# A feed-forward net in three-pass float32: block-product chunks that add onto sums in PSUM, one weight sum made by adding transfers, and one more such chunk in the first net

## The chip, the cores and the metric

The kernel runs on one core of one Trainium2 chip. The metric is the time of one execution on the device in microseconds (us); lower is better. The median of three runs is compared.

## The reference, cut to what matters

Two layers of a small model on 256 tokens of width 1024, all float32. Each layer has two gated feed-forward nets, a token mixer and an attention over 256 memory rows, each followed by a layer norm. The change touches the four feed-forward nets alone.

```python
D_FF = 2816
def swiglu(x, w_gate, w_up, w_down):
    return (jax.nn.silu(x @ w_gate) * (x @ w_up)) @ w_down
for l in range(2):
    h = layer_norm(ALPHA * h + 0.5 * swiglu(h, ffn1_gate[l], ffn1_up[l], ffn1_down[l]), ...)
    ...   # mixer, attention over mem
    h = layer_norm(ALPHA * h + 0.5 * swiglu(h, ffn2_gate[l], ffn2_up[l], ffn2_down[l]), ...)
```

## The kernel before

A product of float32 values is made on TensorE (PE) in three passes: every operand is split into a high part (rounded to the float32r type) and a low part (the rest), and `high*high`, `high*low` and `low*high` are summed in PSUM. `split` (L60 to L62) makes the parts: a cast on ScalarE (ACT, L61) and a subtraction on VectorE (DVE, L62). All weights pass through it: SP loads a tile `raw` of 128x1024 (six buffers), ACT writes `whi`, DVE writes `wlo` (eight buffers each), and PE multiplies with them. So DVE can be at most eight tiles ahead of PE. One weight tile serves 12 matmuls of 512 columns in a plain chunk, and 6 in a block-product chunk.

A net walks over the 2816 hidden columns in chunks: five of 512 and a last one of 256. For a plain chunk (`hidden`), gate and up products take 96 matmuls; `activate` and `gated` leave `silu(gate)*up` in `sg`, and `turn` brings it into the layout that the down product wants, by four transfers (`dealt`), two transposes on DVE and a split. The down product of a chunk is done in two halves by `both(c, u)`, 24 matmuls each, one and two chunks later: at chunk `c` the kernel issues `both(c - 2, 1)` and `both(c - 1, 0)`.

A block-product chunk (`by_seven`, L568 on) treats gate and up of one chunk as four blocks: two halves of the 1024 input columns by gate and up, and the 256 tokens as two tiles of 128. It takes the four block results out of seven products instead of eight, so 84 matmuls instead of 96. For that it needs sums of weight blocks (L597, four sums, each of two 128x1024 tiles, made in place on DVE), sums of input blocks (`blocks_of_x`, once per net), and sums of the seven results (`put`, L619, on DVE). `w00`, `w01`, `w11` and `w10` are the blocks as loaded. Chunks 2 and 4 of a net are of this kind (`sevens`), but in the first net of the first layer (`early` given) only chunk 4.

The first net is special in another way: its chunks 1 and 2 are laid beside the preparation of the memory rows. The memory lands in the tiles `spare0` and `spare1` (32 small transfers issued by POOL, L193), is transposed on DVE (L202) and split into `mT`; small parameters come in through `spare2` and are worked out with some twenty small DVE instructions. `spare0`, `spare1`, `spare2`, `lng` and `lnb` are also the tiles in which `by_seven` puts weight blocks.

The order of instructions on each engine is fixed when the program is built, by a list scheduler with a model of its own; on the chip every engine runs its list strictly in order, and waits where an operand is late. `tc.issue_after` ties the preparation work to places in the list.

Of the kernel before, what the change touches and what calls it, by code (L numbers as in the profile page):

```python
# [17 lines left out]
P = 128  # L18
# [28 lines left out]
def model(ctx: ExitStack, tc: tile.TileContext, t: dict, out: bass.AP):  # L47
# [16 lines left out]
    def load(src, k0, nk, c0, ncol, fine=False):  # L64
# [4 lines left out]
        for a in range(k0, k0 + nk, step):  # L69
# [6 lines left out]
            for b in range(0, step, part):  # L76
                loads.append(nc.sync.dma_start(
                    raw[b // half][:, b % half : b % half + part, :],
                    src[(a + b) * P : (a + b + part) * P, c0 : c0 + ncol].rearrange("(k p) c -> p k c", p=P),
                ))  # L80
# [21 lines left out]
    def product(o, w, x, start, stop):  # L102
        x = x.rearrange("p (h c) -> p c h" if len(x.shape) == 2 else "p r (h c) -> p r c h", h=2)
        o = o.rearrange("p (c h) -> p c h" if len(o.shape) == 2 else "p r (c h) -> p r c h", h=2)
        nc.tensor.matmul(o, w, x, start=start, stop=stop)  # L105
# [23 lines left out]
    def mm_rows(o, xh, xl, wh, wl, start, stop):  # L129
        product(o, xh, wh, start, False)  # L130
        product(o, xh, wl, False, False)
        product(o, xl, wh, False, stop)
# [50 lines left out]
    def load_memory(mp, behind):  # L183
# [14 lines left out]
        def later():  # L198
            for n in range(2):
                for k in range(0, 4, 2):  # L200
                    turned = mp.tile([P, 2, SEQ], F32, tag="up", name="turned")
                    nc.vector.transpose(  # L202
                        turned.rearrange("p k t -> p (k t)"), m[n][:, k : k + 2].rearrange("p k b j -> p (k b j)")
                    )
                    d = slice(4 * n + k, 4 * n + k + 2)
                    split(mTh[:, d, :], mTl[:, d, :], turned)
# [193 lines left out]
    def ffn(l, name, n, pend=None, last=False, early=None):  # L400
        gate, up, down = (t[f"{name}_{x}"][l] for x in ("gate", "up", "down"))
        with tc.tile_pool(name="ffn", bufs=2, reuse_waits="tile") as fp:
# [24 lines left out]
            def ordered(v):  # L427
                return v.rearrange("p (a k j) -> p k a j", a=4, j=32)

            def by_two(v, o):  # L430
                o = o.rearrange("p (n a j m) -> p m n a j", n=2, a=4, m=2)
                return [(ordered(v)[:, 2 * m : 2 * m + 2], o[:, m]) for m in range(2)]

            def activate(s, i, og):
                for v, o in by_two(s[:, i, :], og):
                    nc.scalar.activation(v, o, AF.Silu)

            def gated(s, i, ou):
                for v, o in by_two(s[:, i, :], ou):
                    nc.vector.tensor_tensor(v, o, v, op=ALU.mult)  # L440
# [5 lines left out]
            def turn(s):  # L446
                ah, al = act_tiles()
                x = fp.tile([P, 4, NT, P], F32, tag="dealt", name="dealt", bufs=1)
                for a in range(4):
                    nc.sync.dma_start(x[a * 32 : a * 32 + 32], s[:, :, a * P : (a + 1) * P])  # L450
                for i in range(NT):
                    d = fp.tile([P, 4, P], F32, tag="up", name="square")
                    nc.vector.transpose(
                        d.rearrange("p k (b r) -> p b k r", b=4), x[:, :, i, :].rearrange("p b (k j) -> p b k j", k=4)
                    )
                    split(ah[:, :, tok(i)], al[:, :, tok(i)], d)
# [111 lines left out]
            def by_seven(c0, bx):  # L568
# [19 lines left out]
                w00 = block(gate, 0, pieces("spare0", "spare1"))  # L588
                w01 = block(up, 0, pieces("lng", "lnb"))
# [20 lines left out]
                def run(o, x, w):  # L610
                    for k in range(4):
                        wh, wl = w.at(k, slice(0, CHUNK))
                        mm_rows(o, x[0][:, k, :], x[1][:, k, :], wh, wl, k == 0, k == 3)

                def half_sum():
                    return fp.tile([P, 4, P], F32, tag="up", name="half").rearrange("p k t -> p (k t)")

                def put(o, a, op, b):
                    nc.vector.tensor_tensor(halves(o), sums(a), halves(b), op=op)  # L619

                s = activations()
                g = [s[:, i, :] for i in range(NT)]
                o = [acc((P, CHUNK)) for _ in range(4)]
                run(o[0], part_of_x(0, 0), parts_of(w00))
                nc.scalar.copy(halves(g[0]), sums(o[0]))
                run(o[2], bx[0], parts_of(w00, w01))
                run(o[1], bx[1], parts_of(w00, w11))
                e = half_sum()
                put(e, o[1], ALU.add, g[0])
                run(o[3], bx[2], parts_of(w01, w11))  # L630
                put(g[1], o[3], ALU.add, e)
                f = half_sum()
                put(f, o[2], ALU.subtract, g[1])
                put(e, o[2], ALU.subtract, e)
                o = [acc((P, CHUNK)) for _ in range(3)]
                run(o[0], bx[3], parts_of(w11))
                run(o[1], part_of_x(0, 1), parts_of(w10))
                run(o[2], part_of_x(1, 1), parts_of(w00, w10))


                def left():
                    put(e, o[0], ALU.add, e)
                    for i in range(NT):
                        put(g[i], o[1 + i], ALU.add, g[i])
                    s = fp.tile([P, NT, CHUNK], F32, tag="spare2", name="sg", bufs=1)
                    for i, u in enumerate((e, f)):
                        v = ordered(s[:, i, :])
                        nc.scalar.activation(v, g[i].rearrange("p (k a j) -> p k a j", a=4, j=32), AF.Silu)
                        nc.vector.tensor_tensor(v, v, u.rearrange("p (k a j) -> p k a j", a=4, j=32), op=ALU.mult)
# [571 lines left out]
```

## Time and profile before

| | |
|---|---|
| median of three runs | 1071.56 us (1070.53 to 1072.04) |
| span of the profiled execution | 1068.8 us |
| median less that span | 2.8 us (1071.56 - 1068.8) |
| TensorE busy / its granted clock | 99% of the span / 0.998 |
| VectorE, ScalarE, GpSimd busy | 89%, 60%, 6% |
| DMA queue of SP | 228.49 MB, 64.8% of 16 engines |

The profile is of one execution. A matmul's row is longer than the time it keeps the engine from starting the next one, because matmuls are pipelined; the distance between starts is what counts, and the chain of waits gives it per stage. Views used: the page, the list of waits, the chain of waits in order of time, the timeline of one engine (start, duration, instruction, how many merged, and the idle time before it with what ended it), the groups by line and shape, busy time by stretches (windows), and the DMA issues.

### The profile page before, as it was taken

How to read it: one execution, taken by the hardware profiler on the slowest of the kernel's cores; microseconds unless marked ns; L12 is line 12 of the kernel's file. 1: busy time of each engine (PE TensorE's matmuls, PEld its weight loads, DVE VectorE, ACT ScalarE, POOL GpSimd, SP SyncE). 2: the span in 40 equal slices, each digit the busy share in tenths (PEclk: the TensorE clock that was granted, in tenths of full speed). 3: DMA queues.
4: the chain of work that ended last, by engine and by line, in shares of the span. 5: the costliest groups of instructions: out<-in, count | busy, mean ns of one | idle time of the engine just before them, and what ended most of it. 6: DMA issues, size and time to landing. Idle time of an engine off the chain costs nothing.

```text
span 1068.8 us, 16312 instructions
## 1 busy us (share of the span) xinstructions
PE 1059.3 (99%) x5966; PEld 937.7 (88%) x5966; DVE 946.3 (89%) x1318; ACT 642.4 (60%) x916; POOL 66.4 (6%) x114
## 2 busy tenths in 40 slices
PE   9999999999999999999999999999999999999997
PEld 7888888889899888888888888888898998888886
DVE  6977997998988799999799999788989787999996
ACT  7555664666557565656575557566764665656660
POOL 9700001000000000000000000010000000000000
PEclk9999999999999999999999999999999999999999
DMA  9997484755574575848675865856536665759461
GB/s 362 262 307 256 129 288 165 249 176 174 170 278 167 178 252 194 290 167 218 238 272 184 256 254 183 290 179 216 196 126 213 241 227 181 257 156 334 134 223 40
DMA packets 130895, 231.90 MB, mean 217 GB/s; under 512 B 9408, under 2 KB 48608, under 8 KB 130816
## 3 DMA queue, kind: packets, MB, share of 16 engines
q1 hardware_dynamic: 129024, 228.49, 64.8%
q0 software_dynamic: 1216, 1.20, 0.5%
q8 instruction: 47, 0.77, 0.3%
q10 hardware_dynamic: 576, 1.18, 0.3%
q14 instruction: 32, 0.26, 0.1%
HBM read 216.15 MB, written 1.05 MB: 203 GB/s over the span
## 4 chain that ended last, share of the span: by engine, by line
PE 99%; DMA 0%; DVE 0%; issue 0%; DVEq 0%
PE acc L105 65%; PE dn L105 31%; PE acc L172 1%; PE dn L923 1%; PE dn L982 0%; DMA h<-in_x_dram 0%; PE acc L491 0%; PE dn L981 0%; PE dn L971 0%; PE acc L1047 0%; PE dn L888 0%; DVE h L358 0%; DVE h L353 0%; PE dn L472 0%; DVE st L338 0%
## 5 line engine op out<-in xcount | busy, mean ns | idle before, releaser
L61 ACT CAST whi<-raw 128x1024 fp32r<-128x1024 f32 (+1 forms) x438 | 442.9, 1042 | 197.5 <-DVE raw L597 54.9
L62 DVE TENSOR_TENSOR wlo<-raw,whi 128x1024 fp32r<-128x1024 f32 (+1 forms) x438 | 515.7, 1209 | 32.6 <-ACT whi L61 29.0
L105 PE MATMUL acc<-whi,xT 128*128 128x512 f32 x1032 | 312.9, 380 | 0.0
L105 PEld LDWEIGHTS acc<-whi,xT 128*128 128x128 f32 x1032 | 195.1, 189 | 27.5
L105 PE MATMUL acc<-wlo,xT 128*128 128x512 f32 x516 | 195.6, 379 | 0.0
L105 PE MATMUL acc<-xT,whi 128*128 128x512 f32 x576 | 142.3, 383 | 0.2
L105 PE MATMUL dn<-whi,ah 128*128 128x512 f32 x346 | 131.5, 380 | 0.0
L105 PE MATMUL dn<-wlo,ah 128*128 128x512 f32 x346 | 131.2, 379 | 0.0
L105 PE MATMUL dn<-whi,al 128*128 128x512 f32 x346 | 131.2, 379 | 0.0
L105 PEld LDWEIGHTS acc<-xT,whi 128*128 128x128 f32 x576 | 104.0, 190 | 12.5 <-ACT whi L61 0.7
L105 PEld LDWEIGHTS acc<-wlo,xT 128*128 128x128 f32 x516 | 97.5, 189 | 13.8
L105 PE MATMUL dn<-whi,xT 128*128 128x512 f32 x288 | 87.9, 381 | 0.0
L105 PEld LDWEIGHTS acc<-xT,wlo 128*128 128x128 f32 x576 | 75.5, 191 | 3.9
L105 PE MATMUL acc<-xT,wlo 128*128 128x256 f32 x576 | 75.9, 275 | 0.0
L105 PEld LDWEIGHTS dn<-whi,al 128*128 128x128 f32 x346 | 65.4, 189 | 9.2
L105 PEld LDWEIGHTS dn<-wlo,ah 128*128 128x128 f32 x346 | 65.4, 189 | 9.2
L105 PEld LDWEIGHTS dn<-whi,ah 128*128 128x128 f32 x346 | 65.4, 189 | 9.1
L350 POOL TENSOR_TENSOR rs<-rs,nhalf 128x1 f32<-128x1 f32 x16 | 14.9, 930 | 833.6 <-DVE rs L346 598.1
L597 DVE TENSOR_TENSOR raw<-raw 128x1024 f32<-128x1024 f32 x56 | 66.2, 1217 | 0.4
L105 PEld LDWEIGHTS dn<-whi,xT 128*128 128x128 f32 x288 | 54.4, 189 | 7.7 <-DVE xT L62 0.3
L105 PE MATMUL dn<-wlo,xT 128*128 128x512 f32 x144 | 54.6, 379 | 0.0
L332 DVE SCALAR_TENSOR_TENSOR h<-h,dn 128x512 f32<-128x512 f32 x31 | 21.2, 683 | 32.9 <-PE dn L105 32.9
(234 smaller groups left out, 1277.5 us busy)
## 6 DMA issues: line engine op xcount, KB each, us to landing
raw<-in_ffn_up_dram SPq DMA_DIRECT2D x88, 512.0 KB, 5.3
raw<-in_ffn_down_dram SPq DMA_DIRECT2D x88, 512.0 KB, 6.6
raw<-in_ffn_gate_dram SPq DMA_DIRECT2D x84, 512.0 KB, 5.1
raw<-in_w_in_dram SPq DMA_DIRECT2D x48, 512.0 KB, 4.7
dealt<-sg SPq DMA_DIRECT2D x80, 128.0 KB, 4.7
raw<-in_ca_k_dram SPq DMA_DIRECT2D x16, 512.0 KB, 4.9
raw<-in_w_out_dram SPq DMA_DIRECT2D x16, 512.0 KB, 4.5
raw<-in_ca_v_dram SPq DMA_DIRECT2D x16, 512.0 KB, 5.3
```

What stands on the lines that cost most here:

```text
L61: nc.scalar.copy(hi, src)
L62: lows.append(nc.vector.tensor_tensor(lo, src, hi.bitcast(F32), op=ALU.subtract))
L105: nc.tensor.matmul(o, w, x, start=start, stop=stop)
L172: nc.tensor.transpose(pt[:, k, :], src[:, (4 * j + k) * P : (4 * j + k + 1) * P], unit)
L332: nc.vector.scalar_tensor_tensor(v, v, ALPHA / scale, sums(y[i][n]), op0=ALU.mult, op1=ALU.add, accum_out=None if junk is None else st[:, ...
L350: nc.gpsimd.tensor_tensor(rs, rs, nhalf[:, 0:1], op=ALU.pow)
L597: nc.vector.tensor_tensor(r[i], r[i], plus[i], op=ALU.add)
L923: nc.tensor.matmul(o[g, hh, :], kc[:, hh, g], x, start=True, stop=True)
```

## The change

It does five things.

1. In `by_seven`, products that end in the same result are added in PSUM: one bank is written by four of the seven products and read three times in between by ACT copies (`taken`), a second one is written by two. `put` is left with three uses instead of seven. Matmuls onto a bank that was read must come after that read.
2. The last weight sum, `w00 + w10`, is made by two adding transfers that POOL issues (`accum_op=ALU.add`): they read the `w10` rows from HBM a second time and add them onto `w00` in SBUF.
3. The first net's chunk 3 becomes a block-product chunk too: `sevens` is `(3, 4)` there. `w00` and `w01` swap homes from one such chunk to the next.
4. `both(c - 2, 1)` is issued inside `by_seven`, between the fifth and the sixth product, and `both(c - 1, 0)` before the chunk is finished (`left`).
5. The rows of the down weights are dealt out so that the results can be read in another order; `activate`, `gated` and the split in `turn` become one instruction where they were two. The tile tag `up` has one buffer of 128x1024 instead of two of 128x512, and `turned` (the transposed memory) uses it.

```diff
@@ load
-    def load(src, k0, nk, c0, ncol, fine=False):
+    def load(src, k0, nk, c0, ncol, fine=False, dealt=False):
+                if dealt:
+                    c, u = divmod(a // 2, 2)
+                    at = slice(c * CHUNK + 2 * P * b, c * CHUNK + 2 * P * (b + 1))
+                    rows = src[at, c0 : c0 + ncol].rearrange("(p u) c -> p u c", u=2)[:, u, :]
+                    loads.append(nc.sync.dma_start(to[:, 0, :], rows))
@@ load_memory, later
-                    turned = mp.tile([P, 2, SEQ], F32, tag="up", name="turned")
+                    turned = mp.tile([P, NT, CHUNK], F32, tag="up", name="turned", bufs=1)[:, 0, :]
@@ ffn
-                for v, o in by_two(s[:, i, :], og):
-                    nc.scalar.activation(v, o, AF.Silu)
+                nc.scalar.activation(ordered(s[:, i, :]), in_order(og), AF.Silu)
@@ turn
+                d = fp.tile([P, NT, 4, P], F32, tag="up", name="square", bufs=1)
                 for i in range(NT):
-                    d = fp.tile([P, 4, P], F32, tag="up", name="square")
                     nc.vector.transpose(
...
-                    split(ah[:, :, tok(i)], al[:, :, tok(i)], d)
+                split(*(y.rearrange("p k (i t) -> p k i t", i=NT) for y in (ah, al)), d)
@@ by_seven
+                homes = [("spare0", "spare1"), ("lng", "lnb")]
+                turn_of = sevens.index(c0 // CHUNK) % 2
...
-                o = [acc((P, CHUNK)) for _ in range(4)]
-                run(o[0], part_of_x(0, 0), parts_of(w00))
-                nc.scalar.copy(halves(g[0]), sums(o[0]))
-                run(o[2], bx[0], parts_of(w00, w01))
-                run(o[1], bx[1], parts_of(w00, w11))
-                put(e, o[1], ALU.add, g[0])
-                run(o[3], bx[2], parts_of(w01, w11))
-                put(g[1], o[3], ALU.add, e)
-                put(f, o[2], ALU.subtract, g[1])
-                put(e, o[2], ALU.subtract, e)
-                o = [acc((P, CHUNK)) for _ in range(3)]
-                run(o[0], bx[3], parts_of(w11))
-                run(o[1], part_of_x(0, 1), parts_of(w10))
-                run(o[2], part_of_x(1, 1), parts_of(w00, w10))
+                o = [acc((P, CHUNK)) for _ in range(2)]
+                run(o[0], part_of_x(0, 0), parts_of(w00))
+                taken(s[:, 0, :], o[0])
+                run(o[1], bx[0], parts_of(w00, w01))
+                run(o[0], bx[1], parts_of(w00, w11), True)
+                for i in range(2):
+                    k = 4 + 2 * i
+                    nc.gpsimd.dma_start(
+                        w00[i], gate[k * P : (k + 2) * P, c0 : c0 + CHUNK].rearrange("(k p) c -> p k c", p=P),
+                        accum_op=ALU.add,
+                    )
+                taken(e, o[0])
+                o.append(acc((P, CHUNK)))
+                run(o[2], part_of_x(0, 1), parts_of(w10))
+                run(o[0], bx[2], parts_of(w01, w11), True)
+                put(s[:, 0, :], o[2], ALU.add, s[:, 0, :])
+                nc.scalar.activation(s[:, 0, :], s[:, 0, :], AF.Silu)
+                taken(f, o[0])
+                between()
+                put(f, o[1], ALU.subtract, f)
+                run(o[1], bx[3], parts_of(w11), True)
+                run(o[0], part_of_x(1, 1), parts_of(w00), True)
                 def left():
-                    put(e, o[0], ALU.add, e)
-                    for i in range(NT):
-                        put(g[i], o[1 + i], ALU.add, g[i])
...
+                    activate(s, 1, o[0])
+                    put(e, o[1], ALU.subtract, e)
+                    nc.vector.tensor_tensor(s, s, ef, op=ALU.mult)
                     return turn(s)
@@ ffn
-            sevens = (2, 4) if early is None else (4,)
+            sevens = (2, 4) if early is None else (3, 4)
@@ chunk loop
                 if c > 0:
-                    if c > 1:
+                    if c > 1 and c not in sevens:
                         both(c - 2, 1)
+                    if c < len(chunks) - 1:
+                        both(c - 1, 0)
                     if c in sevens:
                         acts.append(left())
-                    if c < len(chunks) - 1:
-                        both(c - 1, 0)
```

More of the change, by code (lines that the diff above doesn't have):

```diff
@@ L586, in block @@
                     return to
-                w00 = block(gate, 0, pieces("spare0", "spare1"))
-                w01 = block(up, 0, pieces("lng", "lnb"))
+                homes = [("spare0", "spare1"), ("lng", "lnb")]
+                turn_of = sevens.index(c0 // CHUNK) % 2
+                w00 = block(gate, 0, pieces(*homes[turn_of]))
+                w01 = block(up, 0, pieces(*homes[1 - turn_of]))
                 w11 = block(up, 1, pieces("raw", "raw"))
@@ L638, in by_seven @@
[L638 to L649 removed]
+                ef = fp.tile([P, NT, CHUNK], F32, tag="up", name="halves", bufs=1)
```

62 lines of the change are left out of this document (31 added, 31 removed).

## The prediction

> **What bounds the kernel now.** I read the page first, then the list of waits for TensorE (PE), then the chain of waits in order of time, then the VectorE (DVE) timeline of the stages that the change rebuilds.
>
> ```profile
> span 1068.8 us, 16312 instructions
> PE 1059.3 (99%) x5966; PEld 937.7 (88%) x5966; DVE 946.3 (89%) x1318; ACT 642.4 (60%) x916; POOL 66.4 (6%) x114
> PEclk9999999999999999999999999999999999999999
> ```
>
> ```profile
> PE dn L472 <- DVE kTh L467: 1.5, 1, 1.5
> PE acc L491 <- DMA h<-in_x_dram: 0.5, 1, 0.5
> ```
>
> PE waits for 2.0 us in the whole run, all of it at the start. Everything else is issue of matmuls at full clock. So only fewer matmuls can shorten the run, and any wait put on PE lengthens it by its full length. The chain gives the rate (start, length, count):
>
> ```profile
> 75.27 10.36 PE dn L105 x48
> 85.63 20.72 PE acc L105 x96
> 106.35 10.36 PE dn L105 x48
> 116.71 18.13 PE acc L105 x84
> 134.84 10.36 PE dn L105 x48
> ```
>
> 18.13/84 is 0.216 us a matmul. These are the first net's chunk 3 (plain, 96 matmuls from 85.63, then two down halves) and chunk 4 (block products, 84 from 116.71). PE never waits here, but DVE only just keeps up. Its timeline in chunk 4:
>
> ```profile
> 99.75 1.22 DVE L62 TENSOR_TENSOR wlo<-raw,whi 128x1024 fp32r<-128x1024 f32 x1 [0.51 <-ACT whi L61]
> ...
> 115.08 2.36 DVE L597 TENSOR_TENSOR raw<-raw 128x1024 f32<-128x1024 f32 x2
> 117.35 1.30 DVE L453 STREAM_TRANSPOSE square<-dealt 128x512 f32<-128x512 f32 x2
> 118.57 1.19 DVE L62 TENSOR_TENSOR wlo<-raw,whi 128x1024 fp32r<-128x1024 f32 x1
> 119.67 1.28 DVE L62 TENSOR_TENSOR al<-square,ah 128x512 fp32r<-128x512 f32 x2
> 120.88 5.76 DVE L62 TENSOR_TENSOR wlo<-raw,whi 128x1024 fp32r<-128x1024 f32 x5
> 126.55 0.69 DVE L619 TENSOR_TENSOR half<-acc,sg 128x512 f32<-128x512 f32 x1
> 127.15 2.35 DVE L62 TENSOR_TENSOR wlo<-raw,whi 128x1024 fp32r<-128x1024 f32 x2
> 129.42 0.69 DVE L619 TENSOR_TENSOR sg<-acc,half 128x512 f32<-128x512 f32 x1
> 130.02 1.22 DVE L62 TENSOR_TENSOR wlo<-raw,whi 128x1024 fp32r<-128x1024 f32 x1
> ```
>
> The row at 99.75 splits this chunk's first tile: ready at 100.97, wanted at 116.71, a lead of 15.7 us. The row at 130.02 splits the first tile of the down half behind the 84 products: ready at 131.24, wanted at 134.84, a lead of 3.6. One block-product chunk has eaten 12 us of DVE's lead, because a tile there keeps PE busy for 6 matmuls (1.3 us) but costs DVE a subtraction and more than half an addition. Between them DVE is never idle. The steps from start to start are what I count with: 5.67/5 = 1.135 for a 128x1024 subtraction, 2.27/2 = 1.135 for an addition, 0.60 for a 128x512 one, 1.22 for a pair of transposes.
>
> **The change part by part.** *Matmuls.* The first net's chunk 3 drops from 96 to 84: 12 x 0.216 = 2.6 us off PE. The other block-product chunks keep their 84. This is the whole gain on the path, since no other stage has PE idle time to win back.
>
> *DVE.* Each block-product chunk loses two additions (2 x 1.135) and four of seven `put`s (4 x 0.60), about 4.7 us with the merged instructions. In the six chunks of the other three nets, where DVE was never late before, that is more lead and worth nothing. In the first net, chunk 3 gains 6 splits and 6 additions (13.6 us), and stands directly in front of chunk 4, which used to begin with the full lead. So I count DVE's list, in its built order, against PE.
>
> The count starts where before and after are alike, at the memory's transposes:
>
> ```profile
> 66.20 1.30 DVE L202 STREAM_TRANSPOSE turned<-m 128x512 f32<-128x512 f32 x2
> 67.43 1.19 DVE L62 TENSOR_TENSOR wlo<-raw,whi 128x1024 fp32r<-128x1024 f32 x1
> 68.53 1.28 DVE L62 TENSOR_TENSOR mT<-turned,mT 128x512 fp32r<-128x512 f32 x2
> 69.73 1.30 DVE L202 STREAM_TRANSPOSE turned<-m 128x512 f32<-128x512 f32 x2
> 70.95 1.18 DVE L62 TENSOR_TENSOR wlo<-raw,whi 128x1024 fp32r<-128x1024 f32 x1
> 72.06 1.29 DVE L62 TENSOR_TENSOR mT<-turned,mT 128x512 fp32r<-128x512 f32 x2
> 73.26 3.49 DVE L62 TENSOR_TENSOR wlo<-raw,whi 128x1024 fp32r<-128x1024 f32 x3
> 76.67 1.41 DVE L440 TENSOR_TENSOR sg<-acc,sg 128x256 f32<-128x256 f32 x4
> ```
>
> Stretch A, from 66.20 to the second tile of chunk 3's `w00`: four transposes (2.44), four `mT` subtractions (2.4), four splits and two additions (6.8), two `gated` instructions (1.2), 12.9 us in all, so 79.1. But `spare0` and `spare1`, where `w00` lands, hold the memory until it is transposed, and `turned` now has one buffer, so each transpose waits for the cast and subtraction of the one before. The last transpose ends near 73.6; SP can only then issue the second `w00` load; two down tiles stand behind the first one in SP's queue. With the row for such a load, and for the cast that follows it,
>
> ```profile
> raw<-in_ffn_gate_dram SPq DMA_DIRECT2D x84, 512.0 KB, 5.1
> m<-in_mem_dram POOLq DMA_DIRECT2D x32, 32.0 KB, 5.8
> ```
>
> ```profile
> L61 ACT CAST whi<-raw 128x1024 fp32r<-128x1024 f32 x430 | 438.2, 1049 | 197.2 <-DVE raw L597 54.9 <-PE dn L105 53.5 <-PE acc L105 35.5
> L625 ACT COPY sg<-acc 128x512 f32<-128x512 f32 x7 | 4.1, 579 | 0.0
> ```
>
> 73.6 + 5.1 + 1.05 + 1.135 = 80.9; the load may be a little quicker, and I take 80.7. It cannot be under 77.0: in the built order the two `gated` instructions stand in front, the second needs the `up` products of chunk 2, which end at 75.27, and takes 0.60 before the 1.135.
>
> Stretch B, from there to the first down tile that PE uses inside chunk 4. The built DVE list holds 29 subtractions, 10 additions and one product of 128x1024 (40 x 1.135 = 45.4), four transposes (2.44), four `put`s (2.4) and 15 tiny parameter instructions. Those filled, with two splits (2.27), the time between these rows, so they cost up to 1.9; I take 1.5:
>
> ```profile
> 89.93 0.18 DVE L268 COPY prm<-acc 128x32 f32<-128x32 f32 x1
> ...
> 94.14 2.36 DVE L62 TENSOR_TENSOR wlo<-raw,whi 128x1024 fp32r<-128x1024 f32 x2
> ```
>
> Sum 51.7. One microsecond more for waits on ScalarE (ACT), which now does three copies a chunk in its queue of casts, one of them behind the table load for the parameters' `Exp`: 52.7. The tile is ready at 80.7 + 52.7 = 133.4.
>
> PE would want it at 85.63 + 28.49 (84 + 48 matmuls of chunk 3) + 10.36 (four products of chunk 4) = 124.5. The built PE order puts three matmuls of that down half ahead of the fifth product, so PE stands still for them. PE therefore loses 133.4 - 124.5 = 8.9 us over the two chunks. Bounds: 77.0 + 51.7 = 128.7 gives 4.2; 2 us more of waits on DMA or ACT give 10.9. Behind this point chunk 5 restores the lead, as before.
>
> *PE on ACT's copies.* A product that adds onto a bank waits for the copy out of it, with one product (12 x 0.216 = 2.6 us) to hide it. A cast already begun (1.05) and the copy (0.58) fit. In the first net's chunk 3 the copy stands behind casts that wait for DVE's additions, so this wait comes out of the same 8.9. In chunk 2 of the later nets the copy stands behind a cast that needs a buffer PE frees 1.3 us into that product: 1.3 + 1.05 + 0.58 = 2.9, 0.3 too late, but the built order has two matmuls of another product in between (0.43). Zero, bounded by two such places in three chunks, 6 x 0.3 = 1.8.
>
> *The adding transfers.* Each waits on POOL for DVE's last split of the old `w00`; behind it on POOL stand only the layer norms' powers (L350), due much later. Before ACT casts the sum, DVE has 12 instructions in between, some 12 us in every chunk. The trace has no adding transfer; its neighbours land in 5.1 (512 KB, SP) and 5.8 us (32 KB, POOL). I take twice 5.1, hidden, so nothing. If the cover fails, each microsecond beyond 12 counts eight times.
>
> *Edits with one answer.* Merged `activate`, `gated` and `turn` splits save fixed costs on DVE and ACT, off the path. The dealt down rows keep 4 KB runs. `lng` and `lnb` load later, behind the last `w00` split, still over 15 us before use. Moving `both` keeps PE's count and gives DVE a rest in mid chunk; it is in the count.
>
> Sum: 1068.8 - 2.6 + 8.9 = 1075.1 for the span, 1077.9 by the median's offset of 2.8. I say 1078.0.
>
> **Rivals.** *Lead suffices (faster).* If DVE's tiles came in time, the 2.6 us would stand: 1069.0. For it: DVE idles several times before 86 us. Against: its list is strictly ordered, and even the floor above leaves 4.2 us. It decides only if stretch B costs under 43 us. *Small stall.* Between the floor and a little below (2 to 4.5 us lost), within 0.2% of before: 1071.5. It needs quick landings and no ACT waits. *The clock drops.* A long gap could cost PE its rate, as at the start of the run, where five matmuls of 512 columns took
>
> ```profile
> 1.52 2.50 PE L472 MATMUL dn<-kTh 128*128 128x512 f32 x5 [1.52 <-DVE kTh L467]
> ```
>
> 0.50 us each. The gap at 124.5 is one of about 3 us or more; some 16 matmuls at twice 0.216 would add 3.5: 1081.5. [...] *Adding transfers late.* At 15 us each, 3 x 8 = 24 us more: 1102. POOL issued its 32 loads while DVE was nearly saturated and they landed in 5.8, so I give it little.
>
> **How the numbers follow.** About 0.2% (2.1 us) is what can be told from no change here. The forecast 0.64, clock drop 0.11, adding transfers 0.05: slower 0.80. Small stall 0.10: same. Lead suffices 0.10: faster. The range reaches from the floor of the forecast with its quickest landings, 1071.56 - 2.6 + 4.2 = 1073.2, rounded down to 1072.5, to 1082.5, which holds the clock drop and the 1.8 of the copies; outside are the faster case and the late transfers.
>
> **What would show it.** Right: PE waits of 6 to 11 us in all between 88 and 140 us, named by DVE `wlo` (L62) or ACT; DVE without idle time from 66 to 133; from there on the chain as before, shifted; PE 12 matmuls shorter. In the other nets no PE wait over 0.3. Wrong: no PE wait in that stretch (lead suffices), ACT casts waiting on the adding transfers, or a granted clock below 1 there.

## The result, and the profile after

The changed kernel takes 1079.9 us (median of 4, 1079.7 to 1084.1), the kernel before in the same runs 1071.8 (1070.5 to 1072.5): a ratio of 1.0088, 95% interval 1.0072 to 1.0105. It is slower by 8.1 us. The prediction was 1078.0 in a range of 1072.5 to 1082.5. The profiled execution took 1079.9, 2.0 above its span. Its page:

```profile
span 1077.9 us, 16241 instructions
PE 1060.8 (98%) x5954; PEld 936.5 (87%) x5954; DVE 927.7 (86%) x1237; ACT 652.9 (61%) x893; POOL 85.8 (8%) x130
```

DVE has 18.6 us less to do in the whole run, PE has 12 matmuls fewer and is still 1.5 us longer busy; the reason for that comes below. The list of PE's waits (total, times, longest) had 2.0 us at the start and nothing else before. Now:

```profile
PE acc L112 <- ACT sg L635: 4.0, 3, 3.2
PE acc L112 <- DVE wlo L62: 1.9, 1, 1.9
PE acc L112 <- ACT halves L635: 1.6, 3, 0.7
PE dn L479 <- DVE kTh L474: 1.5, 1, 1.5
PE acc L498 <- DMA h<-in_x_dram: 0.5, 1, 0.5
```

Three new lines. Two of them name the copies (L635) out of a bank onto which the next product adds. PE's timeline shows the waits of the first net one by one (start, length, and in brackets the idle time before it with its releaser):

```profile
90.75 0.38 PE L112 MATMUL acc<-whi,kTl 128*128 128x512 f32 x1
94.31 0.48 PE L112 MATMUL acc<-whi,kTh 128*128 128x512 f32 x1 [3.18 <-ACT sg L635]
...
122.90 0.38 PE L112 MATMUL acc<-whi,xT 128*128 128x512 f32 x1
125.17 0.48 PE L112 MATMUL acc<-wlo,xT 128*128 128x512 f32 x1 [1.89 <-DVE wlo L62]
...
126.60 0.63 PE L112 MATMUL acc<-wlo,kTh 128*128 128x512 f32 x1
127.03 0.63 PE L112 MATMUL acc<-whi,kTl 128*128 128x512 f32 x1
```

From 90.75 to 94.31 is one step of 3.56 where 0.216 is usual: 3.3 us lost in chunk 3 (3.4 with the slow first step behind it). From 122.90 to 125.17 another 2.1 (2.2) in chunk 4. Then, from 126.54 on, the trace's record of the granted clock stands at half for 3.41 us, and matmuls follow each other at 0.43: 1.7 us more. PE counts as busy in these. It also counts as busy for some 0.27 us more at each gap, an estimate from the rows: 0.38 instead of 0.216 ahead of the gap, and a step of 0.32 behind it. That is why its busy time grew. The first net loses 7.3 us in all.

Why the first copy is late is read from ScalarE (ACT) and DVE in chunk 3:

```profile
88.56 1.22 DVE L606 TENSOR_TENSOR raw<-raw 128x1024 f32<-128x1024 f32 x1
```

```profile
89.89 1.99 ACT L61 CAST whi<-raw 128x1024 fp32r<-128x1024 f32 x2 [3.50 <-PE acc L112]
91.79 1.04 ACT L61 CAST ah<-square 128x1024 fp32r<-128x1024 f32 x1
92.73 1.04 ACT L61 CAST whi<-raw 128x1024 fp32r<-128x1024 f32 x1
93.68 0.57 ACT L635 COPY sg<-acc 128x512 f32<-128x512 f32 x1
```

The product that fills the bank ended at about 88.5. But the copy stands on ACT behind four casts, and the first of these needs the sum that DVE's addition ends at 89.78. (The row names PE as the releaser; the addition ended 0.1 us before the cast began.) So the wait at the copy is a wait for DVE at one remove. The view by stretches (length, then busy time and count of PE, PEld, DVE, ACT and POOL, then PE's clock, the share of the DMA engines and GB/s) says the same for the stage. First the kernel before, from 86 to 125 us:

```profile
86.00:125.00 39.00, 39.00 (x183) 34.15 (x182) 36.34 (x52) 25.27 (x31) 0.00 (x0) 1.00 0.51 174
```

Now the changed kernel:

```profile
48.00:63.00 15.00, 15.00 (x71) 13.13 (x70) 8.26 (x9) 6.29 (x6) 1.65 (x3) 1.00 1.07 295
63.00:86.00 23.00, 23.00 (x108) 20.10 (x107) 20.91 (x24) 11.04 (x14) 0.00 (x0) 1.00 0.73 255
86.00:125.00 39.00, 34.10 (x157) 29.21 (x155) 38.96 (x51) 28.45 (x33) 4.30 (x4) 1.00 0.66 202
```

From 86 to 125 DVE is now busy for 38.96 of 39.00 us and PE for only 34.10. From 48 to 63 DVE is idle for 6.7 of 15 us.

The later nets lose 4.0 us, 1.34 to 1.36 in each, at two places of chunk 2: at the product that waits for the first copy out of the bank (into `sg`) and at the one that waits for the second (into `halves`). In the kernel before, the chain of waits (start, length, what) is PE alone there, here in the second net:

```profile
415.80 18.13 PE acc L105 x84
```

Now it leaves PE twice:

```profile
417.20 0.61 DVE sg L445
...
417.83 0.61 SPq L455
...
419.16 0.61 SPq L455
...
419.81 6.22 DMA dealt<-sg
...
426.14 0.59 ACT sg L635
...
426.78 3.73 PE acc L112 x16
...
432.06 0.58 ACT halves L635
...
432.69 2.86 PE acc L112 x12
```

The first time it runs through the chunk ahead: its activations in the single buffer `sg` are finished at 417.81, four transfers (L455, 0.61 us each on SP's queue) deal them out, the last has read them at 426.0, and only then may ACT copy the first product into the same buffer. In the old form the bank of that copy was next written by the fifth product, three products later. But ACT's own list shows that this buffer costs little here:

```profile
420.18 5.78 ACT L61 CAST whi<-raw 128x1024 fp32r<-128x1024 f32 x6 [4.69 <-DVE raw L606]
426.14 0.59 ACT L635 COPY sg<-acc 128x512 f32<-128x512 f32 x1 [0.18 <-DMA dealt<-sg]
...
428.27 1.05 ACT L61 CAST ah<-square 128x1024 fp32r<-128x1024 f32 x1 [0.60 <-DVE square L458]
429.22 2.94 ACT L61 CAST whi<-raw 128x1024 fp32r<-128x1024 f32 x3
432.06 0.57 ACT L635 COPY halves<-acc 128x512 f32<-128x512 f32 x1
```

The bank was full at about 423.4. The copy stands behind six casts, one right behind the other from the moment at which DVE's sum is there until 425.96; the buffer holds it for 0.18 us more. The second copy's bank was full at about 429.6, and it stands behind four casts, the first of which needed DVE's transposes. In the third net the buffer holds the first copy for 0.26 us, in the fourth not at all, and the fourth loses as much as the others:

```profile
949.18 5.78 ACT L61 CAST whi<-raw 128x1024 fp32r<-128x1024 f32 x6 [4.69 <-DVE raw L606]
954.87 0.59 ACT L635 COPY sg<-acc 128x512 f32<-128x512 f32 x1
```

So by these rows at most 0.4 of the 4.0 us is the buffer's. The rest is casts that stand ahead of the copies on ACT and begin late, because the first of each row waits for DVE's sum or transposes.

### The profile page after: what moved, and what is told of

Read it like the earlier page. It is cut to its first block, busy times and chain, and to the rows that moved or that the text cites. A ratio compares the mean times of both kernels' runs of the same rounds, so it can differ in the third digit from the quotient of the medians.

```text
span 1077.9 us, 16241 instructions
## 1 busy us (share of the span) xinstructions
PE 1060.8 (98%) x5954; PEld 936.5 (87%) x5954; DVE 927.7 (86%) x1237; ACT 652.9 (61%) x893; POOL 85.8 (8%) x130
## 4 chain that ended last, share of the span: by engine, by line
PE 79%; DVE 10%; DMA 5%; issue 3%; ACT 1%; SPq 1%; DVEq 0%; ACTq 0%
PE acc L112 50%; PE dn L112 26%; DVE wlo L62 5%; DMA dealt<-sg 2%; DVE raw L606 1%; DMA raw<-in_ffn_up_dram 1%; PE acc L179 1%; ACT whi L61 1%; SPq L455 1%; DVE sg L445 1%; PE dn L938 1%; DVE quarters L571 0%; DVE al L62 0%; DMA raw<-in_ffn_gate_dram 0%; DVE kTl L62 0%
## 5 line engine op out<-in xcount | busy, mean ns | idle before, releaser
L62 DVE TENSOR_TENSOR wlo<-raw,whi 128x1024 fp32r<-128x1024 f32 (+1 forms) x444 | 524.7, 1208 | 63.8 <-ACT whi L61 50.3
L61 ACT CAST whi<-raw 128x1024 fp32r<-128x1024 f32 (+1 forms) x444 | 449.9, 1042 | 209.0 <-PE dn L112 63.8
L112 PE MATMUL acc<-whi,xT 128*128 128x512 f32 x992 | 302.6, 380 | 0.0
L112 PEld LDWEIGHTS acc<-whi,xT 128*128 128x128 f32 x992 | 187.6, 189 | 26.6
L112 PE MATMUL acc<-wlo,xT 128*128 128x512 f32 x496 | 188.1, 379 | 1.9 <-DVE wlo L62 1.9
L112 PEld LDWEIGHTS acc<-wlo,xT 128*128 128x128 f32 x496 | 93.8, 189 | 15.4 <-DVE wlo L62 2.3
L606 DVE TENSOR_TENSOR raw<-raw 128x1024 f32<-128x1024 f32 x48 | 57.1, 1215 | 0.4
L112 PE MATMUL acc<-whi,kTh 128*128 128x512 f32 x128 | 49.8, 389 | 5.6 <-ACT sg L635 4.0
```

Of the source, the lines that this page charges most:

```text
L61: nc.scalar.copy(hi, src)
L62: lows.append(nc.vector.tensor_tensor(lo, src, hi.bitcast(F32), op=ALU.subtract))
L112: nc.tensor.matmul(o, w, x, start=start, stop=stop, skip_group_check=more)
L606: nc.vector.tensor_tensor(r[i], r[i], plus[i], op=ALU.add)
```

## The experiments

Theory A, mine: the two block-product chunks in a row are more than DVE can feed, so PE loses what DVE is short of, wherever it then stands; copies cost only what is not covered. Theory B: the new form itself costs, because products that add onto a bank wait for ACT's copies. Theory C came up after the fourth run.

All results, from one profile each. "Lost" is what PE's longer steps (from start to start) take beyond 0.216 us, from 60 to 140 us and from 140 to 184 (the net's end), the half clock included; "half clock" is half the time that the clock's record stands at half. "Later nets" is the same sum over their chunks, of steps over 0.31 us; the kernel before has none so long there. In experiments 2, 6, 8, 10 and 12 the profiled execution was the longest of its kernel's, 0.7 to 1.9 us above the median.

| kernel | median us | ratio to before, 95% interval | lost 60-140 | lost 140-184 | half clock | later nets |
|---|---|---|---|---|---|---|
| before | 1071.8 | | 0.1 | 0.1 | 0 | 0 |
| after | 1079.9 | 1.0088 [1.0072, 1.0105] | 7.3 | 0.1 | 1.7 | 4.0 |
| 1 chunk 3 plain | 1075.5 | 1.0044 [1.0029, 1.0059] | 0.1 | 0.1 | 0 | 4.1 |
| 2 old form | 1087.3 | 1.0152 [1.0137, 1.0167] | 14.8 | 3.5 | 3.4 | 0.1 |
| 3 no sums | 1076.8 | 1.0056 [1.0039, 1.0073] | 2.3 | 0.1 | 0 | 4.1 |
| 4 copy first | 1084.3 | 1.0125 [1.0110, 1.0140] | 6.9 | 0.1 | 0 | 8.9 |
| 5 more cover | 1082.0 | 1.0102 [1.0087, 1.0117] | 11.2 | 0.5 | 3.4 | 2.3 |
| 6 vector sum | 1083.9 | 1.0118 [1.0101, 1.0135] | 12.3 | 0.4 | 3.4 | 4.1 |
| 7 transfer sum | 1081.3 | 1.0100 [1.0085, 1.0115] | 8.3 | 0.5 | 1.7 | 2.3 |
| 8 GpSimd sum | 1087.6 | 1.0155 [1.0140, 1.0170] | 15.6 | 0 | 5.1 | 4.0 |
| 9 memory later | 1080.6 | 1.0089 [1.0075, 1.0103] | 1.4 | 6.1 | 1.7 | 4.1 |
| 10 combined | 1080.6 | 1.0083 [1.0069, 1.0097] | 2.7 | 7.7 | 1.7 | 2.4 |
| 11 memory early | 1074.8 | 1.0044 [1.0029, 1.0058] | 2.9 | 0.1 | 0 | 4.1 |
| 12 all together | 1075.7 | 1.0037 [1.0024, 1.0051] | 6.3 | 0.1 | 1.7 | 2.4 |

### 1. Chunk 3 plain again

```
-            sevens = (2, 4) if early is None else (3, 4)
+            sevens = (2, 4) if early is None else (4,)
```

> The changed kernel, but in the first net only chunk 4 is made of block products; chunk 3 is plain again (96 matmuls). Theory A (two such chunks in a row use up VectorE's lead): the first net's losses of 7.3 us (3.4 at the copy, 2.2 at the tile, 1.7 at the lower clock) go, 12 matmuls come back (2.6), and the three later nets keep their 4.0 of waits on copies: 1079.9 - 7.3 + 2.6 = 1075.2. Theory B (the form itself costs: a product that adds onto a bank waits for ScalarE's copy, whatever the lead): chunk 4 of the first net still waits for its copies, 1.3 as in a later net up to 3.4 as in chunk 3: 1076.5 to 1078.6.

Measured 1075.5. Its list of waits, beside the two at the start:

```profile
PE acc L112 <- ACT halves L635: 1.7, 3, 0.8
PE acc L112 <- ACT sg L635: 0.6, 1, 0.6
```

All of these lie in the later nets; the first net has no wait. The same form, copies and adding transfers in chunk 4 cost nothing when a plain chunk stands in front. Theory A holds for the first net, and the copies of the later nets are a matter of their own.

### 2. The old form in two chunks in a row

The kernel before, with `sevens = (2, 4) if early is None else (3, 4)`.

> The kernel before with one edit: the first net's chunk 3 is a block-product chunk in the old form (no adding onto PSUM sums, no adding transfers, no copies that PE waits for). Theory A: VectorE has some 4.7 us more work in each of the two chunks than in the changed kernel, so PE loses about 7.3 + 9 = 16 us in the first net and nothing in the later nets: 1071.8 - 2.6 + 16 = 1085. Theory B: without copies to wait for, only the wait on the tile and the lower clock (2.2 + 1.7) are left: about 1073.

Measured 1087.3, and no copy in the list:

```profile
PE acc L105 <- DVE wlo L62: 4.9, 6, 1.6
PE acc L105 <- ACT whi L61: 4.5, 5, 2.1
```

With 4.7 us more DVE work in each of the two chunks, the first net loses 18.3 instead of 7.3. Theory B's 1073 is far off. The rewritten form is the better one by over 7 us if chunk 3 is to be a block-product chunk at all.

### 3. DVE's sums of chunk 3 left out

```
-                        if plus is not None:
+                        if plus is not None and not (early is not None and c0 == 3 * CHUNK):
```

> The changed kernel, but the six additions of weight blocks in the first net's chunk 3 are left out (its products take the blocks unsummed; splits, products, copies and transfers stay). Theory A: VectorE has 6 x 1.135 = 6.8 us less in front of chunk 4, so at most 1 us of the first net's 7.3 us is left: 1079.9 - 6.3 = 1073.6, with no slow matmuls. Theory B: the copy out of the bank stands in the same ScalarE queue, its wait of 3.4 us stays: 1079.9 - 3.9 = 1076.0.

In the profiled execution (1074.4) the loss falls from 7.3 to 2.3, without half clock, and the wait at chunk 3's copy is gone altogether, though the copy and its place remain. So it was DVE's additions that held the casts in front of it. The remainder is larger than the 1 us expected, at chunk 4's first w10 tile. The five runs lie between 1074.4 and 1079.7, and their median, 1076.8, is nearer to theory B's 1076.0 than to A's 1073.6; for A speaks the trace, in which the wait that B keeps is not there.

### 4. The copy moved forward on ACT

```
-                        split(h, w, r[i])
+                        with tc.issue_after(copies[-1].ins) if behind and i else nullcontext():
+                            split(h, w, r[i])
```

`behind` is set for the weights of the two products that add onto the first bank, so the second cast of each stands behind the copy.

> The changed kernel; in every block-product chunk the second cast of the weights that the waiting product itself needs is put behind the copy in ScalarE's queue, so the copy comes earlier. Theory A: the later nets' 4.0 us go; in the first net the total loss stays at 6 to 8 us, because VectorE's work is the same: the wait moves from the copy to a tile in chunk 4. 1079.9 - 4.0 = 1075.9. Theory B: the first net's 3.4 us at the copy go as well: 1072.5.

Slower by 4.4 us than the changed kernel. In the first net A's number held: 6.9 lost against 7.3, moved to seven smaller waits, four of them on tiles. In the later nets both theories missed: 8.9 lost instead of 4.0. The group of ACT's copies into `sg` (count, busy, mean, then idle time in front and its releasers), first of the changed kernel, then of this one:

```profile
L635 ACT COPY sg<-acc 128x512 f32<-128x512 f32 x8 | 4.7, 586 | 0.4 <-DMA dealt<-sg 0.4
```

```profile
L638 ACT COPY sg<-acc 128x512 f32<-128x512 f32 x8 | 4.7, 584 | 42.3 <-DMA dealt<-sg 32.7 <-PE acc L112 9.6
```

ACT now stands idle for 42.3 us in front of them instead of 0.4, with casts queued behind. The copy could not come much earlier: its target was still being dealt out. So in the changed kernel the casts and the buffer let the first copy go at nearly the same time, and taking away one of the two is not enough.

### 5. More work between copy and waiting product

```
                 run(o[1], bx[0], parts_of(w00, w01))
+                run(o[2], part_of_x(0, 1), parts_of(w10))
                 run(o[0], bx[1], parts_of(w00, w11), True)
...
                 taken(e, o[0])
+                between(0)
-                run(o[2], part_of_x(0, 1), parts_of(w10))
                 run(o[0], bx[2], parts_of(w01, w11), True)
                 taken(f, o[0])
-                between()
+                between(1)
```

> The changed kernel with its products in another order: the w10 product stands between the first copy and the product that waits for it, and 24 down matmuls (5.2 us) stand behind each of the two other copies. Nothing is added or left out. Theory A (VectorE's lead is the first net's limit, a copy costs only what the work between does not cover): the later nets' 4.0 us of waits on copies go to under 0.5; the first net still loses 6 to 8 us, at a tile and no longer at the copy: 1079.9 - 3.7 = 1076.2. Theory C (put up after the run in which the copy was moved forward and the waits moved to the tiles: in the later nets casts and splits have no slack at all in chunk 2, so that any order waits): about 4 us stay there, at tiles: 1080.

Theory C is out: in chunk 2 of the later nets not one wait is left, and the chain there is PE alone again (4.0 less). New waits, the longest 0.4 on ACT's cast `ah` of chunk 5's own activations, appear at the end of the nets (2.3 in all), so the gain is 1.7 in place of the 3.7 that A gave. The first net got worse, 11.2 for 7.3, and 1.7 of the difference is more time at half clock. The median lies above both forecasts. The longest wait of PE is now on a down tile, inside chunk 4:

```profile
PE dn L112 <- ACT whi L61: 3.8, 1, 3.8
```

That tile's cast stands on ACT behind casts of sums, and ACT stood idle for 5.08 us in front of these until DVE had added. DVE in turn waited 0.86 and 1.00 us for loads of the `up` weights. So "6 to 8, at a tile and no longer at the copy" was too neat: an order can waste DVE's time.

### 6. The adding transfers undone

```
-                for i in range(2):
-                    k = 4 + 2 * i
-                    nc.gpsimd.dma_start(
-                        w00[i], gate[k * P : (k + 2) * P, c0 : c0 + CHUNK].rearrange("(k p) c -> p k c", p=P),
-                        accum_op=ALU.add,
-                    )
...
-                run(o[0], part_of_x(1, 1), parts_of(w00), True)
+                run(o[0], part_of_x(1, 1), parts_of(w00, w10), True)
```

> The changed kernel with its adding transfers undone: VectorE adds w10 onto w00 (two additions a block-product chunk more, 16 in all). Theory A: the two in the first net's chunk 3 stand in front of the late tiles and cost 2 x 1.135 = 2.3 us, those of chunk 4 up to as much more, those of the later nets nothing: 1082.2 to 1084.4. Rival (the adding transfers land late and casts wait for them): 1078 to 1080.

Measured 1083.9, the upper half of what A gave. The adding transfers are worth 4 us; no wait of PE in the list names them. On the page of the changed kernel they land in 7.0 us.

### 7. A second sum by adding transfers

Against experiment 5:

```
+                for i in range(2):
+                    k = 4 + 2 * i
+                    nc.gpsimd.dma_start(
+                        w01[i], up[k * P : (k + 2) * P, c0 : c0 + CHUNK].rearrange("(k p) c -> p k c", p=P),
+                        accum_op=ALU.add,
+                    )
                 run(o[2], part_of_x(0, 1), parts_of(w10))
...
-                run(o[0], bx[2], parts_of(w01, w11), True)
+                run(o[0], bx[2], parts_of(w01), True)
```

> The kernel of more cover, and the sum w01 + w11 made by adding transfers too, as w00 + w10 is: two additions a chunk less on VectorE. Theory A: 2 to 4 additions less in front of the late tiles in the first net, 2.3 to 4.5 us less lost there: 1076.2 - 2.3 to - 4.5 = 1071.7 to 1073.9, and nothing in the later nets. Rival (a 512 KB adding transfer took 7.0 us to land, and the cast of the sum waits for it): no gain or slower, 1076 to 1080, with casts on ScalarE that wait for a transfer.

1081.3, above both forecasts and 0.7 less than experiment 5, where 2.3 to 4.5 less were expected. The trace lost 8.3 instead of 11.2. DVE had four additions less to do but stood idle for the loads of chunk 4's `up` weights:

```profile
114.54 2.48 DVE L606 TENSOR_TENSOR raw<-raw 128x1024 f32<-128x1024 f32 x2 [2.95 <-DMA raw<-in_ffn_up_dram]
```

### 8. A sum by GpSimd

```
-                run(o[0], bx[2], parts_of(w01, w11), True)
+                run(o[0], bx[2], parts_of(w01, w11, nc.vector if early is None else nc.gpsimd), True)
```

> The changed kernel, and in the first net alone the sum w01 + w11 (four 128x1024 additions) made by GpSimd instead of VectorE. Theory A: as much less on VectorE as it loses additions: 2.3 to 4.5 us less lost, 1075.4 to 1077.6. Rival (GpSimd is slow at it, or slows VectorE beside it, and the adding transfers on its queue are issued later): no gain, 1079 to 1084.

The slowest of all, above both forecasts. POOL's timeline and DVE's:

```profile
84.22 3.23 POOL L606 TENSOR_TENSOR raw<-raw 128x1024 f32<-128x1024 f32 x1 [3.49 <-DVE raw L606]
...
121.16 3.23 POOL L606 TENSOR_TENSOR raw<-raw 128x1024 f32<-128x1024 f32 x1 [2.35 <-DVE raw L606]
```

```profile
85.28 4.38 DVE L62 TENSOR_TENSOR wlo<-raw,whi 128x1024 fp32r<-128x1024 f32 x2
...
122.08 3.39 DVE L606 TENSOR_TENSOR raw<-raw 128x1024 f32<-128x1024 f32 x1
```

An addition that takes DVE 1.21 takes POOL 3.23 in three of the four cases (2.38 in the first, at 78.35), and DVE's instruction beside it grows from 1.21 to as much as 3.39. DVE gains little time, if any, and the sum comes later.

### 9. The memory behind the two chunks

```
-                    if bx:
-                        rest[1]()
-                    else:
+                    if not bx:
                         bx.extend(blocks_of_x())
...
                     gb = ln_params(l, n)
+                    if early is not None:
+                        with tc.issue_after(lows[-1].ins):
+                            rest[1]()()
...
-        return parameters, load_memory(op, made)
+        return parameters, lambda: load_memory(op, made)
```

> The changed kernel; the loading of the memory and its four transposes, casts and subtractions are moved from the first net's chunks 1 and 2 to its chunk 5, behind both block-product chunks. Theory A (VectorE's work ahead of the late tiles sets the first net's loss): 4 x 0.61 + 4 x 0.60 = 4.9 us of VectorE's work leave that stretch, so of 5.6 us of waits and 1.7 us of lower clock 0.7 to 2.4 are left: 1079.9 - 5.0 to - 6.6 = 1073.3 to 1075. Rival (the stretch behind chunk 4 has no more room than the one in front, and the memory is wanted soon after): waits reappear past 140 us, 1076 to 1080.

Each was right about its own stretch. Up to 140 us 1.4 us is left of 7.3, as A said. But it comes back at the net's end, where the memory is now turned between the layer norm's steps, and the median is just above the rival's 1076 to 1080:

```profile
PE acc L179 <- DVE h L365: 2.7, 1, 2.7
PE dn L112 <- DVE wlo L62: 1.1, 1, 1.1
```

### 10. Three edits together

Experiment 9, with the sum by transfers of experiment 7 in the first net and the order of experiment 5 in the later nets:

```
+                if early is None:
+                    o = [acc((P, CHUNK)) for _ in range(3)]
...
+                    run(o[2], part_of_x(0, 1), parts_of(w10))
...
+                    between(0)
...
+                else:
...
+                    run(o[0], bx[2], parts_of(w01), True)
```

> The changed kernel with the memory moved to chunk 5, the first net's sums w01 + w11 made by adding transfers as well, and the later nets in the order with more cover for the copies. Theory A: nothing is left of the first net's 7.3 us, and of the later nets' 4.0 some 1.5 as in the run with more cover: 1079.9 - 7.3 - 2.5 = 1070.1, level with the kernel before or a little under it. Rival (the added transfers and the later memory bring waits of their own, past 100 us): 1073 to 1076.

1080.6, above both forecasts: the later nets gain 1.6 as in experiment 5, the first net's end loses 7.7. Taking DVE's work out in front does not help while it is short behind.

### 11. The memory ahead of the two chunks

```
-    turned = mp.tile([P, NT, CHUNK], F32, tag="up", name="turned", bufs=1)[:, 0, :]
+    turned = wp.tile([P, DM], F32, tag="lng" if k else "lnb", name="turned")[:, 0:512]
```

> The changed kernel with one edit: the memory's transposes write to the buffers lng and lnb, which are free then, and no longer through the single buffer that the chunks' turned activations use too; so their 4.9 us of VectorE's work can go into its idle times between 48 and 63 us, ahead of the stretch that runs late. Theory A (VectorE's work between 63 us and the late tiles sets the first net's loss, and work moved out of it to either side frees PE): as with the memory moved behind chunk 4, about 1 us of the 7.3 is left before 140 us, but now nothing comes back at the net's end: 1079.9 - 6.1 = 1073.8, and with nothing left at all 1072.6. Rival (the first net is short of VectorE as a whole): part of it comes back past 140 us, 1075 to 1079.

1074.8, 5.1 us less than the changed kernel, for another place of the turned memory; it lies between A's 1073.8 and the rival's 1075. The same three stretches again:

```profile
48.00:63.00 15.00, 15.00 (x72) 13.12 (x71) 12.27 (x16) 8.20 (x10) 1.75 (x4) 1.00 1.06 298
63.00:86.00 23.00, 23.00 (x109) 20.11 (x108) 22.22 (x23) 11.60 (x13) 1.60 (x2) 1.00 0.73 261
86.00:125.00 39.00, 36.83 (x170) 31.70 (x169) 37.77 (x50) 28.39 (x33) 3.25 (x3) 1.00 0.77 222
```

DVE does 4.0 us more before 63, where it used to stand idle, and from 86 to 125 PE is busy for 36.83 us in place of 34.10. The profile has 2.9 us lost in the first net where A expected about 1, no half clock, and nothing at the net's end, so but for that rest the first net was not short of DVE as a whole. It had put the work in the wrong place, because one buffer was shared by the memory and the chunks' activations. (The edit also gives the memory two buffers in turn. The kernel before had two, shared with the activations, and turned the memory at 66.20 as well; so the sharing is the likelier cause, but no run parts the two.)

### 12. Everything that helped

Experiment 11, with the later nets and the second sum as in experiment 10, no w10 matmul ahead of the product that waits for the copy, and in chunk 4 the copy ahead of that product's last cast:

```
+                    copy = taken(s[:, 0, :], o[0])
...
+                    done = run(o[0], bx[1], parts_of(w00, w11, copy if c0 == 4 * CHUNK else None), True)
...
+                    with tc.issue_after(done.ins):
+                        run(o[2], part_of_x(0, 1), parts_of(w10))
```

> The kernel of the memory turned early, and with it: in the first net the sums w01 + w11 by adding transfers (four additions less on VectorE), no w10 matmuls ahead of the product that waits for the copy, and in chunk 4 the copy ahead of the last cast of that product; in the later nets the order with more cover for the copies. Theory A (VectorE's work between 63 us and the late tiles, and cover for the copies, are all that is lost): of the 2.6 us left in the first net under 1, of the later nets' 4.0 some 1.5: 1074.8 - 1.6 to - 2.6 - 2.5 = 1069.7 to 1070.7, level with the kernel before or just under it. Rival (the order of casts and transfers costs again what the additions save, as where copies were moved forward or sums made by transfers before): 1073 to 1076.

1075.7, not better than experiment 11, as the rival said. The later nets gained 1.7; in the profiled execution the first lost 3.4 more, half of it at half clock. The copy in chunk 4, moved forward, met the same wall as in experiment 4:

```profile
122.78 0.58 ACT L637 COPY sg<-acc 128x512 f32<-128x512 f32 x1 [5.37 <-DMA dealt<-sg]
```

No version beat the kernel before. A second buffer for `sg` together with a copy moved forward was not tried; by the rows of the result section the buffer by itself would take off at most 0.4 us.

## Why the prediction was right, and where it was not

The result lies in the range, and in the first net the mechanism was the forecast one: DVE's late list holds up PE. But the terms of the sum are not those that I named, and part of the agreement is luck.

*Matmuls.* 12 fewer, 5966 to 5954, 2.6 us: as said.

*DVE's ledger.* It held to about 1 us. The second tile of chunk 3's `w00` was to be ready at 80.7, the first down tile inside chunk 4 at 133.4. The first was split at 81.8. The second is the first of the four in this row, 132.74 + 1.22 = 133.96:

```profile
132.74 4.62 DVE L62 TENSOR_TENSOR wlo<-raw,whi 128x1024 fp32r<-128x1024 f32 x4
```

*The wait.* The 8.9 us were to fall at that tile. They did not: PE had lost 5.6 at two places upstream (the copy in chunk 3, the w10 tile in chunk 4) and 1.7 to the clock. The step that failed is where PE first meets the late list, and what it needs there. I had taken the built order's three down matmuls for the first trap; three w10 matmuls, put ahead of chunk 4's third product, came earlier. And the three down matmuls read only the tile's high part, which ACT's cast makes, not the low part that I had counted up to 133.4:

```profile
129.75 1.99 ACT L61 CAST whi<-raw 128x1024 fp32r<-128x1024 f32 x2 [1.20 <-DVE raw L606]
```

```profile
131.93 0.81 PE L112 MATMUL dn<-whi,ah 128*128 128x512 f32 x3
```

The second of these casts ended at 131.74, 0.2 us before PE came. The first matmul that needs the low part started at 135.17, 1.2 us after it was ready. In all 7.3 instead of 8.9, well between my bounds (4.2 and 10.9). A PE that had lost nothing upstream would have come to that cast at 124.5, as I had it, and waited about 7.2 us there. That would explain why experiment 4 moved the loss and did not shrink it, but it is argued from the two rows and no run shows it. That a copy in chunk 3 would wait behind casts that wait for additions was foreseen, and counted in the same sum.

*PE on ACT's copies in the later nets.* The place and the kind of the wait were foreseen, two in each of three chunks, a copy behind casts; the size was wrong: zero taken, 1.8 as the bound, 4.0 measured. I had counted one cast ahead of the copy, behind a buffer that PE frees, and 0.3 us too late at each place. The trace has six casts in a row ahead of the first copy and four ahead of the second, each row begun late because of DVE, and 0.24 to 0.90 us lost at each place, with 0.1 more for the slow first step. I also did not ask what the copy's target waits for: the single `sg`, still read by the transfers of the chunk ahead. It cost at most 0.4 in the changed kernel, but it is what kept experiment 4 from winning anything. In the kernel before the same copy had three products of cover; the change left it one.

*The clock.* I gave it 0.11 with 3.5 us more, and named a granted clock below 1 in this stretch as a sign of being wrong. It came, with 1.7. No run ahead of the result shows the 16 slow matmuls of that case; the changed kernel's trace has 8, at 0.43 each (126.60 to 129.59), and the profiles of experiments 2, 5 and 6 lost 3.4 us each at half clock.

*Adding transfers.* Hidden, as said: 7.0 us to land, under the 10.2 that I took. Nothing in the list waits for them.

*The sum.* 1078.0 + 4.0 (copies) - 1.6 (7.3 for 8.9) - 0.8 (2.0 for 2.8 between span and time) = 1079.6, of 1079.9 measured. That is luck in part: the waits of the first net were 5.6 for 8.9, and the clock (1.7) and the copies (4.0), both at zero in the sum, made up for it. Of the span's growth of 9.1, -2.6 + 7.3 + 4.0 = 8.7 is placed, 0.4 is not.

*What would show it.* PE waits of 6 to 11 us between 88 and 140: not quite, 5.1 of waiting, 5.6 with the slow first steps, 7.3 only with the clock. DVE without idle time from 66 to 133: nearly so, 1.95 us idle before 76 and none of note after. "In the other nets no PE wait over 0.3": wrong, 0.35 to 0.73 in five of six places.

## What to carry to other kernels

An engine with idle time on the whole can still set the time of a stage (DVE here, busy for 86% of the span and for 38.96 of the 39.00 us from 86 to 125): count its list between the place where it last had a lead and the place where it next gets one, and look for idle time just ahead of that, and for the buffer that keeps work from moving there. When a product is made to wait for a copy, follow the copy back along everything that it waits for: the work ahead of it in its engine's list, and the buffer that it writes, which the stage before may still read. Here the two came free within 0.3 us of each other, so moving the copy forward gained nothing: an instruction that is put ahead of what it depends on makes everything behind it wait, as the copies of experiment 4 did, with 42.3 us of ACT's idle time in front of them.

## What the runs showed of the hardware

*The clock and the gaps.* In the nine traces with a slow clock in the first net, it lasted 3.41 or 6.83 us. A gap of 3.3 us (changed kernel, 90.97 to 94.31) brought none; one of 2.05 (123.12 to 125.17) did, 1.4 us after it had ended. Within each of these traces all changes of the clock lie whole steps of 3.413 us apart (in the changed kernel's they stand at 7.07, 126.54, 129.95 and 1075.44). I counted back from the start of each slow stretch in such steps, with 0.216 us of work for each matmul that starts. In ten steps at full clock PE was idle for 63 to 94% of the step, and the next one ran slow every time. In nine it was idle for 51 to 59%, and none of these was followed by a slow one; the 3.3 us gap is shared by two steps, with 42 and 59%. A limit between the two is not shown: experiment 11 has a step that was 61% idle without a slow one behind it, and by the busy time of the view by stretches, which counts a matmul's whole row, a step of 55% idle in the changed kernel (1.52 us busy from 123.13 to 126.54) was followed by a slow one and a step of 56% (1.51 from 92.41 to 95.82) was not. So the length of a gap alone did not set its price: in this one trace 3.3 us brought no slow stretch, and 2.05 us brought 1.7 us of loss at half clock. That such stretches make the runs of one kernel differ (1074.4 to 1079.7 in experiment 3, 1073.4 to 1080.2 in experiment 11) is likely, but not shown: each kernel left one trace. In experiment 11 the three runs with a granted clock of 0.997 took 1076.9 us or more and the six at 0.998 or 0.999 took 1075.1 or less; the runs of experiment 10 do not sort that way.

*VectorE beside GpSimd.* Beside POOL's additions of 3.23 us, DVE's instructions with two inputs in SBUF took 2.80, 3.25 and 3.39 instead of 1.21 (experiment 8), and each ended 1.1 us after POOL's addition had ended. The one addition that took POOL 2.38 had no such instruction of DVE beside it until 0.3 us before its end. What held them up, the rows do not say.
